# Attention block on one core: adding transfers moved in the issue order of GpSimd

## The chip, the core and the metric

The kernel runs on one core of a Trainium2 chip. A core has a matrix engine (TensorE, PE in the profile, with its weight loads shown as PEld), a vector engine (VectorE, DVE), an engine for activation functions (ScalarE, ACT), a general engine (GpSimd, POOL) and a queue engine that only issues transfers (SyncE, SP). Each engine takes its own instructions strictly in order, and they wait for each other by semaphores. Data lies in the on-chip memory (SBUF, 128 partitions) and in the accumulation banks of TensorE (PSUM). Sixteen transfer (DMA) engines move data; a transfer is issued by one of the engines' queues, and a transfer that adds to what lies at its destination is issued here by POOL.

The metric is device time of one execution in microseconds (us): 1025.42 us is the median of three runs before the change (1024.97 to 1025.84).

## The reference

One transformer layer over 1024 latent tokens (16 rows of 64) of width 1024, with 256 context tokens. The first half of the layer mixes tokens, half of its width by four pooling windows and half by attention over a neighbourhood of 8 x 16 tokens plus all context tokens, and projects the two halves together:

```python
h_x = _modulate(x, g_pre_mix[l], sh1, sc1)
u_x, q_x, k_x, v_x = _project(h_x, w_in[l])
attn_x = _neighbourhood_attention(q_x, k_x, v_x, k_c, v_c, rpb[l])
mix_x = jnp.concatenate([_pool_mixer(u_x, pool_w[l], pool_scale[l]), attn_x], axis=-1) @ w_out[l]
x = x + gt1 * _rmsnorm(mix_x, g_post_mix[l])
y_x = _sq_relu_mlp(_modulate(x, g_pre_mlp[l], sh2, sc2), w_mlp_in[l], w_mlp_out[l])
x = x + gt2 * _rmsnorm(y_x, g_post_mlp[l])
```

All is float32.

## The kernel before

**Arithmetic.** A float32 product is made as three products of rounded parts: each operand is split in a high part (a cast) and a low part (what the cast left, `low_part`, L175, a DVE instruction that reads two SBUF operands), and TensorE forms high x high, high x low and low x high (L221 to L223). The large projections are further done by a scheme of seven block products instead of eight, whose operands are sums and differences of blocks. Some of those sums are made by adding transfers: `add_to(to, more)` (L211) is a transfer issued by POOL which adds `more` to `to`.

**Stages.** From 0 to some 218 us: modulation, projections of pools, keys, queries and values. From 218 to 317 us: attention. Then the output projection to some 400 us, then the MLP.

**Attention.** There are 32 units: 4 pairs of heads (j) times 8 tiles of 128 tokens (m). The loop runs over i = 0 to 35, and in step i TensorE does in this order: the scores of unit i (L1168, tiles `S`, two buffers of two banks, one for each head e of the pair), the turning of unit i-2 (L1214, transposes of its weights `sp` and of its shares `rb` by multiplication with `ident`, into `T`, `pa`, `pz`), and the weighted values of unit i-3 (L1248). Around that:

- DVE adds the bias table to the scores and takes the row's minimum (L1183, `sp`, `nm`), for e = 0 and 1. Between the two it takes the reciprocal of the row sums of unit i-1 (L1198, `ri`).
- ACT takes the exponential (L1194), copies one half of the turned weights (L1233) and the small side pieces (L1228, `px`); DVE copies the other half (L1233, `pt`).
- POOL spreads the reciprocal over 128 columns (L1200, `rb`). This copy is issued inside `scores(i)` for unit i-1, and TensorE needs it when it turns that unit, in step i+1.
- POOL also builds bias tables (L1037, `tab`, from a loaded table `U`), splits operands (L1050, L1051), and issues transfers.
- DVE multiplies the values by the shares into `heads[j]` (L1258, `weighed`).

In steps 0 and 1 TensorE also finishes the query projection (`last_query("P4", i)`, tiles `pqv`), and in step 1 the queries are split (`query_parts(0, 1)`: ACT L169, DVE L175 with output `qP`).

**The adding transfers.** `pools[k]` (`y` in the profile) are four pages of 1024 columns, `s3[k]` their left and `s1a[k]` their right half. First `s3[k]` gets `s1a[k]` added (k = 0 to 3); SP copies the sums into `sa2[k]` (`ss`, L1403, steps 5 and 6). When pair j of heads is finished, its right half is added to `s1a[j]` and to `sa2[j]` (step 8j+11), and later `sa2[j]` to the left half of `heads[j]` (step 8j+15). Each moves 128 x 512 numbers, 256 KB. The sums are operands of the output projection.

**Order.** The engines' order here is the order in which the code is written: the manager `in_order` ties each instruction of an engine to the one before it (for POOL `first_pool`). So on POOL whatever stands ahead of a `rb` copy in the code is issued ahead of it. In step i the code before the change wrote the adding transfers ahead of `scores(i)`:

```python
if i > 3:
    weighed(i - 4)
    if i % 8 == 3: ...          # two adds of finished heads
...
if i in (1, 2): ...             # two adds each of the pools
if 8 < i < N and i % 8 == 7: ...# one add to the heads
low()
if i < N:
    scores(i)                   # holds the rb copy of unit i-1
```

Of the kernel before, what the change touches and what calls it, by code (L numbers as in the profile page):

```python
# [103 lines left out]
def hybrid_block(ctx, tc, x, ctx_in, w_mod, mod_pages, b_mod, gp1, gp2, w_in, pool_w, rpb, w_out, w1, w2, vectors,  # L104
# [105 lines left out]
    def add_to(to, more):  # L210
        nc.gpsimd.dma_start(to, more, accum_op=add)  # L211
# [82 lines left out]
    with tc.tile_pool(name="ps1", bufs=6, space=PSUM) as ps1, tc.tile_pool(name="tmp1", bufs=3) as tmp:  # L294
# [10 lines left out]
        ET = mybir.EngineType  # L305
# [747 lines left out]
        def part_page(name, spare):  # L1053
            return whl.tile([P, 1024], F32R, tag="hl", name=name) if spare else page(name, F32R)
# [7 lines left out]
        def query_parts(j, b, spare=False, pool=False):  # L1062
            t = part_page(f"qP{j}_{b}", spare)
            qparts[j, b] = t[:, :512], t[:, 512:]
            apart(qT[j][b], *qparts[j, b], pool)
# [73 lines left out]
    with (  # L1139
# [6 lines left out]
        probs, least, sums, shares, turns, turned, fifths, heads = {}, {}, {}, {}, {}, {}, {}, {}  # L1146
# [114 lines left out]
        N = len(units)  # L1261
# [66 lines left out]
        sa2 = [both[k // 2][:, (k % 2) * 512 : (k % 2) * 512 + 512] for k in range(4)]  # L1328

        s3, s1a = [p[:, :512] for p in pools], [p[:, 512:] for p in pools]  # L1330
# [12 lines left out]
        with in_order(ET.PE, ET.Activation, ET.DVE, ET.SP) as projected:  # L1343

            def last_query(n, j):
                half_product(n, "Q", j, last_queries)
                kept_product(n, "Q", j, last_queries[j])

            query_parts(0, 0, True)
            key_parts(0, 1)  # L1350
            query_parts(1, 0, True, True)
            last_query("P7", 0)
            last_query("P7", 1)

            table = [None] + [tables(j) for j in (1, 2, 3)]
            built = lambda j: next(table[j])
            out_of = lambda n: mod_out(n, accs[n])
            jobs = {0: [(built, 1), (key_parts, 1, 0), (key_parts, 1, 1)], 1: [(built, 1)], 2: [(built, 1)], 3: [(built, 1)],
                    4: [(built, 1)], 5: [(out_of, "a")], 6: [(out_of, "sc")], 7: [(query_parts, 1, 1, True, True)],
                    8: [(mixed_split, 0, True)], 9: [(built, 2), (out_of, "sh")],  # L1360
                    10: [(columns_of, "sc", scale2), (built, 2)], 12: [(columns_of, "sh", s2), (built, 2)],
                    13: [(built, 2), (built, 2)], 14: [(query_parts, 3, 0, False, True)],
                    16: [(mixed_split, 1, True)], 17: [(query_parts, 2, 1, True, True)],
                    18: [(built, 3), (key_parts, 3, 0, False, True)], 20: [(built, 3), (built, 3)],
                    21: [(built, 3), (built, 3)], 22: [(key_parts, 3, 1, False, True)], 24: [(mixed_split, 2, True)],
                    25: [(query_parts, 3, 1, False, True)], 26: [(weight_split, 0, True)], 28: [(weight_split, 1, True)],
                    29: [(weight_split, 2, True)], 30: [(weight_split, 3, True)]}
            for i in range(N + 4):
                if i in LOADS:
                    weight_load(0, kks[LOADS.index(i)])  # L1370
                if i == N:
                    t1 = [out_load(f"to1_{kk}w", kk, 1) for kk in (0, 1)]
                    b22 = [out_load(f"bo22_{kk}w", kk, 1) for kk in (2, 3)]
                    t3 = [out_load(f"to3_{kk}w", kk, 1) for kk in (2, 3)]
                    for to, kk in zip(t1, (0, 1)):
                        add_to(halved(to), out_block(kk, 0))
                if i == N - 2:
                    G1 = gate_page("a")
                if i > 3:
                    weighed(i - 4)  # L1380
                    if i % 8 == 3:
                        j = i // 8 - 1
                        add_to(s1a[j], heads[j][:, 512:])
                        add_to(sa2[j], heads[j][:, 512:])

                rest_of_bank = lambda name: pz[:, 256:]
                if i == 0:
                    gain = mod_gain(gp1, att.tile([P, 256], F32, tag="gp", name="gpa"), nc.sync)
                if i == 4:
                    mod_gate("a", accs["a"], gain, rest_of_bank)  # L1390
                    accs["sh"] = page("accsh2")
                    nc.sync.dma_start(accs["sh"], kept_row)
                if i == 5:
                    column_sums("sc", accs["sc"], rest_of_bank)
                if i == 8:
                    column_sums("sh", accs["sh"], rest_of_bank)
                if i in (1, 2):
                    with tc.issue_after(pooling[ET.Pool]):
                        for k in (2 * i - 2, 2 * i - 1):
                            add_to(s3[k], s1a[k])  # L1400
                if i in (5, 6):
                    for k in (2 * i - 10, 2 * i - 9):
                        nc.sync.dma_start(sa2[k], s3[k])  # L1403
                if 8 < i < N and i % 8 == 7:
                    j = i // 8 - 1
                    add_to(heads[j][:, :512], sa2[j])
                low()
                if i == N:
                    mixed_split(3)
                for n, at in enumerate(HALVES):  # L1410
                    if at == i:
                        weight_split(n)
                if i < N:
                    scores(i)
                    for f, *args in jobs.get(i, ()):
                        f(*args)
                else:

                    t = i - N
                    if t == 0:  # L1420
                        x, s1 = [], halves_of("so1_")
                    if t % 2 == 0:
                        xs = ps_s.tile([P, 1024], F32, tag="S", name=f"pox{t}")
                        x += [xs[:, :512], xs[:, 512:]]
                    out_sums(x[t], "A11", wo, t, True)
                    nc.scalar.copy(s1[t], x[t])
                if 1 < i <= N + 1:
                    turn(i - 2)
                    fifth_kept(i - 2)
                if i < N:  # L1430
                    exps(i, 0)
                if 1 < i <= N + 1:
                    turn_kept(i - 2, 0, nc.scalar.copy)
                if i < N:
                    exps(i, 1)
                if i == 0:
                    key_parts(2, 0, True, "lo")
                    key_parts(2, 1, True, "lo")
                    query_parts(2, 0, False, "lo")
                if 1 < i <= N + 1:  # L1440
                    turn_kept(i - 2, 1, nc.vector.tensor_copy)
                if i < 2:
                    last_query("P4", i)
                if i == N:
                    share(i - 1)
                if 2 < i <= N + 2:
                    values(i - 3)
                if i == 1:
                    query_parts(0, 1)
                if i > N:  # L1450
                    out_operand("S1", i - N - 1, s1a[i - N - 1])
            low()
            for t in range(4):
                out_sums(x[t], "A12", [wo[2], wo[3]], t, False)
            t2 = [out_load(f"to2_{kk}w", kk, 1, wraw) for kk in (2, 3)]
            t4 = [out_load(f"to4_{kk}w", kk, 0, wraw) for kk in (2, 3)]
            for i in range(2):
                add_to(t2[i], t1[i])
            add_to(heads[3][:, :512], sa2[3])
            for i in range(2):  # L1460
                add_to(halved(t3[i]), out_block(i, 1))
            for i in range(2):
                add_to(t4[i], t2[i])
            first_pool.__exit__(None, None, None)
            wt1 = [high_low(f"to1_{t}", t1[t]) for t in range(2)]
            junk = lambda t: att.tile([P, NKEY], F32, tag="sp", name=f"jo0_{t}", bufs=6)[:, :512]
            out_operand("S2", 0, sa2[0])
            out_kept(0, 0, x[0], junk(0))
            out_operand("S2", 1, sa2[1])
            out_operand("S1", 3, s1a[3])  # L1470
            out_kept(0, 1, x[1], junk(1))
            out_operand("S2", 2, sa2[2])
            out_operand("S2", 3, sa2[3])
            for t in (2, 3):
                out_kept(0, t, x[t], junk(t))
# [729 lines left out]
```

## Time and profile before

| | us |
|---|---|
| median of three runs | 1025.42 (1024.97 to 1025.84) |
| the profiled execution | 1025.65 |
| its span, first to last instruction | 1023.9 |
| PE busy | 1012.5 (99%) |
| DVE busy | 747.8 (73%) |
| ACT busy | 544.8 (53%) |
| POOL busy | 149.8 (15%) |
| granted clock of TensorE | 0.998 |

How to read it: the profile is one execution. Its busy times of TensorE are partly modelled, since matmuls are pipelined. A row of the timeline gives the start and the length of an instruction (or of several equal ones in a row, "x3"), and in brackets how long the engine had been idle and which instruction ended that wait. The chain that ended last goes back from the last instruction, at each step to what released it. Each `DMA_DIRECT2D` row on POOL is the time in which POOL issued a transfer, not the transfer's own time.

### The profile page before, as it was taken

Reading aid. Unit: us, or ns where it says so; the run is one execution under the profiler, and the core shown is the slowest. Engines: PE = TensorE matmul, PEld = TensorE weight load, DVE = VectorE, ACT = ScalarE, POOL = GpSimd, SP = SyncE. Lnnn points to the kernel's source line nnn. Section 1 sums busy time; section 2 is a strip of 40 time slices with the busy share of each in tenths; the row PEclk is TensorE's granted clock in tenths of the full one; section 3 lists DMA queues with packets and bytes.
Section 4 is the critical chain, followed back from the end, with each engine's and each line's share of the span. In section 5 each row is a group of like instructions: output and inputs, shape, how many; then the busy total and the mean of one; then the engine's idle time right before and its main releaser. Section 6 shows DMA issues by size and latency. Waiting matters only on the chain.

```text
span 1023.9 us, 16144 instructions
## 1 busy us (share of the span) xinstructions
PE 1012.5 (99%) x5962; PEld 838.5 (82%) x5962; DVE 747.8 (73%) x1164; ACT 544.8 (53%) x949; POOL 149.8 (15%) x231
## 2 busy tenths in 40 slices
PE   9999999999999999999999999999999999999997
PEld 7788888878898888888888888888888888888886
DVE  5688657977886688879998888755756666547576
ACT  6683254348886646776555554545543334334431
POOL 3011110156773321410000000000000000000002
PEclk9999999999999999999999999999999999999999
DMA  9899798623347955886776666537967766546555
GB/s 359 321 260 337 246 268 297 206 59 86 86 95 205 228 183 198 272 203 205 262 254 212 214 198 227 183 133 237 347 219 256 259 215 219 204 175 195 166 184 225
DMA packets 117023, 222.72 MB, mean 218 GB/s; under 512 B 9488, under 2 KB 46992, under 8 KB 116944
## 3 DMA queue, kind: packets, MB, share of 16 engines
q1 hardware_dynamic: 90448, 171.14, 49.5%
q0 software_dynamic: 9360, 19.58, 9.4%
q10 hardware_dynamic: 17136, 30.97, 8.1%
q8 instruction: 47, 0.77, 0.3%
q14 instruction: 32, 0.26, 0.1%
HBM read 168.16 MB, written 52.45 MB: 215 GB/s over the span
## 4 chain that ended last, share of the span: by engine, by line
PE 95%; DMA 2%; POOL 1%; ACT 1%; issue 0%; DVE 0%; SPq 0%; DVEq 0%; POOLq 0%; ACTq 0%
PE pu L467 4%; PE pa L1248 4%; PE phz L221 3%; PE phv L221 3%; PE phx L221 3%; PE pyx L221 3%; PE pyx L223 3%; PE phx L223 3%; PE pyv L222 3%; PE pyz L222 3%; PE phz L223 3%; PE pyx L222 3%; PE phv L223 3%; PE pyv L223 3%; PE pyz L223 3%; PE phx L222 3%
## 5 line engine op out<-in xcount | busy, mean ns | idle before, releaser
L1194 ACT ACTIVATE sp<-sp,nm 128x640 f32<-128x640 f32 (+1 forms) x64 | 51.5, 804 | 9.6 <-DVE ri L1198 4.9
L1183 DVE CUSTOM_DVE_ANT_0 sp<-S,tab 128x640 f32<-128x640 f32 (+1 forms) x56 | 44.6, 796 | 14.1 <-PE pz L1214 9.7
L169 ACT CAST wpS<-S 128x512 fp32r<-128x512 f32 x64 | 38.7, 616 | 29.0 <-PE phv L223 10.0
L1790 ACT ACTIVATE c<-c 128x512 f32<-128x512 f32 x48 | 30.3, 631 | 42.9 <-DVE c L1910 25.0
L221 PE MATMUL phx<-thB,wpA 128*128 128x512 f32 x128 | 50.2, 392 | 0.0
L223 PE MATMUL phx<-thB,wpA 128*128 128x512 f32 x128 | 49.8, 389 | 0.0
L222 PE MATMUL phx<-tlB,wpA 128*128 128x512 f32 x128 | 49.8, 389 | 0.0
L175 DVE TENSOR_TENSOR wpS<-S,wpS 128x512 fp32r<-128x512 f32 x64 | 43.5, 688 | 8.4 <-ACT wpS L169 8.4
L163 POOL TENSOR_TENSOR ry<-vy,nhalf 128x1 f32<-128x1 f32 x8 | 5.9, 739 | 281.1 <-DVE vy L161 281.1
L1791 ACT ACTIVATE c<-c 128x512 f32<-128x512 f32 x48 | 30.3, 631 | 15.2 <-DVE sa L1873 12.2
L221 PEld LDWEIGHTS phx<-thB,wpA 128*128 128x128 f32 x128 | 24.0, 188 | 5.4 <-ACT s L1841 0.5
L223 PEld LDWEIGHTS phx<-thB,wpA 128*128 128x128 f32 x128 | 24.0, 188 | 5.1
L222 PEld LDWEIGHTS phx<-tlB,wpA 128*128 128x128 f32 x128 | 24.0, 188 | 4.8
L1233 DVE COPY pt<-T 128x512 f32<-128x512 f32 x32 | 22.0, 686 | 5.8 <-PE T L1214 5.8
L1248 PE MATMUL pa<-pt,v 128*64 128x128 f32 x352 | 25.9, 279 | 0.2
L221 PE MATMUL phz<-thB,wpS 128*128 128x512 f32 x64 | 25.0, 391 | 0.0
L221 PE MATMUL phv<-thT,wpA 128*128 128x512 f32 x64 | 25.0, 391 | 0.0
L223 PE MATMUL phz<-thB,wpS 128*128 128x512 f32 x64 | 24.9, 389 | 0.0
L222 PE MATMUL phv<-tlT,wpA 128*128 128x512 f32 x64 | 24.9, 389 | 0.0
L222 PE MATMUL phz<-tlB,wpS 128*128 128x512 f32 x64 | 24.9, 389 | 0.0
L221 PE MATMUL phy<-thT,wpS 128*128 128x512 f32 x64 | 24.9, 389 | 0.0
L222 PE MATMUL phy<-tlT,wpS 128*128 128x512 f32 x64 | 24.9, 389 | 0.0
(1139 smaller groups left out, 3438.1 us busy)
## 6 DMA issues: line engine op xcount, KB each, us to landing
b<-in_w SPq DMA_DIRECT2D x64, 512.0 KB, 4.2
hrS<-hdS SPq DMA_DIRECT2D x32, 512.0 KB, 5.1
hrA<-hdA SPq DMA_DIRECT2D x24, 512.0 KB, 5.2
wm<-in_mod_pages SPq DMA_DIRECT2D x16, 512.0 KB, 9.6
wa_0w<-in_w SPq DMA_DIRECT2D x16, 512.0 KB, 5.2
wa_1w<-in_w SPq DMA_DIRECT2D x16, 512.0 KB, 4.4
hdA<-c ACTq DMA_DIRECT2D x32, 256.0 KB, 2.4
hdS<-sa ACTq DMA_DIRECT2D x32, 256.0 KB, 2.3
```

The source lines that it names most:

```text
L169: nc.scalar.copy(hi, src)
L175: nc.vector.tensor_tensor(lo, src, hi.bitcast(F32), sub)
L221: nc.tensor.matmul(ps, ahi, bhi, start=first, stop=False, skip_group_check=more)
L222: nc.tensor.matmul(ps, ahi, blo, start=False, stop=False, skip_group_check=more)
L223: nc.tensor.matmul(ps, alo, bhi, start=False, stop=last, skip_group_check=more)
L467: nc.tensor.matmul(pus[b][j], wk(wgt, k, low, j * P, P), r, start=(k == 0 and n == 0), stop=(k == KT - 1 and n == 2))
L1183: nc.vector.tensor_tensor_reduce(out=to, in0=s, in1=bt, scale=1.0, scalar=BIG, op0=add, op1=ALU.min, accum_out=nm)
L1194: nc.scalar.activation(sp, sp, AF.Exp, bias=least[i, e], scale=-1.0, accum_out=sums[i][:, e : e + 1])
L1233: copy(turns[i].rearrange("p e i t -> p (e i) t")[:, :, h * HD : (h + 1) * HD], turned[i][h].rearrange("p (a t) -> p a t", a=8))
L1248: nc.tensor.matmul(pa[e * HD : (e + 1) * HD, cols], v[:, f : f + HD], turns[i][:, e, c] if c < 4 else fifths[i][:, :, (e + 1) * HD : (e + ...
L1790: nc.scalar.activation(r, src, AF.Relu)
L1791: nc.scalar.activation(r, r, AF.Square)
```

## The change

Only POOL's order changes; the instructions, their number and their operands stay. Three groups of adding transfers move:

1. The four adds `s3[k] += s1a[k]` move from steps 1 and 2 to the place ahead of the last query products and of unit 0.
2. The two adds of finished heads in steps 11, 19 and 27 move behind `scores(i)`, which means behind the `rb` copy of unit i-1. (In step 35 there are no scores; they stay.)
3. The add to the left half of the heads in steps 15, 23 and 31 moves likewise.

```diff
             query_parts(1, 0, True, True)
+            with tc.issue_after(pooling[ET.Pool]):
+                for k in range(4):
+                    add_to(s3[k], s1a[k])
             last_query("P7", 0)
             last_query("P7", 1)
+
+            def right_added(j):
+                add_to(s1a[j], heads[j][:, 512:])
+                add_to(sa2[j], heads[j][:, 512:])
...
                     weighed(i - 4)
-                    if i % 8 == 3:
-                        j = i // 8 - 1
-                        add_to(s1a[j], heads[j][:, 512:])
-                        add_to(sa2[j], heads[j][:, 512:])
+                    if i > N and i % 8 == 3:
+                        right_added(i // 8 - 1)
...
-                if i in (1, 2):
-                    with tc.issue_after(pooling[ET.Pool]):
-                        for k in (2 * i - 2, 2 * i - 1):
-                            add_to(s3[k], s1a[k])
...
-                if 8 < i < N and i % 8 == 7:
-                    j = i // 8 - 1
-                    add_to(heads[j][:, :512], sa2[j])
                 low()
...
                     scores(i)
+                    if 8 < i and i % 8 == 3:
+                        right_added(i // 8 - 1)
+                    if 8 < i and i % 8 == 7:
+                        add_to(heads[i // 8 - 1][:, :512], sa2[i // 8 - 1])
```

What this does to POOL's order is seen at two places. The first is around units 0 to 2. Before the change POOL's rows are these (`y` are the pools' pages, `rb` the spread reciprocals of units 0 and 1, `tab` a bias table, `kP2l` and `qP` low parts of keys and queries):

```order
L1024 MEMSET tab_2182 128x256
L1024 MEMSET tab_2183 128x256
L1051 TENSOR_TENSOR kP2l<-kT_1885,kP2h 128x512 x2
L1051 TENSOR_TENSOR qP_0_2204<-q_2_1992,qP_0_2204 128x512
L211 DMA y_1367<-y_1367 128x512
L211 DMA y_1413<-y_1413 128x512
L1200 COPY rb_2241<-ri_2239 128x128
L1037 TENSOR_TENSOR tab_2182<-msk,U_2186 128x128 x3
L211 DMA y_1463<-y_1463 128x512
L211 DMA y_1503<-y_1503 128x512
L1200 COPY rb_2289<-ri_2287 128x128
```

After the change POOL's rows at the same place are these:

```order
L1051 TENSOR_TENSOR qP_0_2128<-q_0_1741,qP_0_2128 128x512
L211 DMA y_1367<-y_1367 128x512
L211 DMA y_1413<-y_1413 128x512
L211 DMA y_1463<-y_1463 128x512
L211 DMA y_1503<-y_1503 128x512
L1024 MEMSET tab_2186 128x256
L1024 MEMSET tab_2187 128x256
L1051 TENSOR_TENSOR kP2l<-kT_1885,kP2h 128x512 x2
L1051 TENSOR_TENSOR qP_0_2208<-q_2_1992,qP_0_2208 128x512
L1200 COPY rb_2243<-ri_2241 128x128
L1037 TENSOR_TENSOR tab_2186<-msk,U_2190 128x128 x3
L1200 COPY rb_2289<-ri_2287 128x128
```

The four issues went ahead of the memsets and of the splits of keys and queries, and nothing stands any more between the last split and the first `rb` copy, and only one table step between the first and the second.

The second place is POOL in step 11, as one piece of the difference (`f` are the finished heads, `sc` and `s` small columns of the modulation that POOL fetches):

```order
 L776 DMA sc_984<-gsc 128x8x1
 L1037 TENSOR_TENSOR tab_2029<-msk,U_2800 128x128 x3
+L1200 COPY rb_2933<-ri_2931 128x128
 L211 DMA y_1367<-f_2394 128x512
 L211 DMA ss_2119<-f_2394 128x512
-L1200 COPY rb_2935<-ri_2933 128x128
 L1200 COPY rb_3002<-ri_3000 128x128
 L776 DMA s_86<-gsh 128x8x1
```

The `rb` copy of unit 10 now goes ahead of the two issues. In steps 19 and 27 the same happens, and in steps 15, 23 and 31 with one issue. The rows of PE, DVE, ACT and SP are the same as before, in the same order.

## The prediction

> **What bounds the kernel now.** I read the page first, then who TensorE waited for over the whole span, then the timelines of PE, POOL and DVE at those waits.
>
> ```profile
> span 1023.9 us, 16144 instructions
> PE 1012.5 (99%) x5962; PEld 838.5 (82%) x5962; DVE 747.8 (73%) x1164; ACT 544.8 (53%) x949; POOL 149.8 (15%) x231
> PE 95%; DMA 2%; POOL 1%; ACT 1%; issue 0%; DVE 0%; SPq 0%; DVEq 0%; POOLq 0%; ACTq 0%
> ```
>
> TensorE is the bound: 95% of the chain that ended last, and only 11.4 us of its span idle. POOL is busy 15%, so moving its work can only pay where TensorE waits for POOL. The list of TensorE's waits names these, for attention:
>
> ```profile
> PE pa L1214 <- POOL rb L1200: 1.8, 3, 0.8
> PE S L1168 <- DVE nm L1183: 0.3, 1, 0.3
> ```
>
> Three waits, 1.8 us in all. PE's timeline shows where (rows before a wait show when PE was done):
>
> ```profile
> 226.96 0.29 PE L1168 MATMUL S<-kch,qP 64*128 64x256 f32 x2
> 227.87 0.27 PE L1214 MATMUL pa<-ident,rb 64*128 64x64 f32 x1 [0.62 <-POOL rb L1200]
> 229.18 0.44 PE L1168 MATMUL S<-kP0h,qP 64*128 64x384 f32 x1 [0.31 <-DVE nm L1183]
> 231.10 0.27 PE L1214 MATMUL pa<-ident,rb 64*128 64x64 f32 x1 [0.77 <-POOL rb L1200]
> 259.52 0.27 PE L1214 MATMUL pa<-ident,rb 64*128 64x64 f32 x1 [0.39 <-POOL rb L1200]
> ```
>
> These are the turnings of units 0, 1 and 10, in steps 2, 3 and 12. The chain shows what stood ahead of POOL's copies for units 0 and 1:
>
> ```profile
> 224.51 1.29 POOL qP L1051
> 225.79 1.72 POOL y L211 x2
> 227.52 0.30 POOL rb L1200
> 227.81 1.21 POOL tab L1037 x3
> 229.02 1.73 POOL y L211 x2
> 230.75 0.31 POOL rb L1200
> ```
>
> and for unit 10:
>
> ```profile
> 257.36 0.92 POOL y L211
> 258.28 0.90 POOL ss L211
> 259.18 0.31 POOL rb L1200
> ```
>
> All three waits end at an `rb` copy directly behind two issues that the change moves. No such wait is listed for steps 15 to 31, so moving those issues is worth nothing; the 0.9 us by which each delayed its copy was covered by TensorE's own work.
>
> **Part 1, the pools' adds.** Their new place on POOL follows the split that ends at 215.24:
>
> ```profile
> 213.53 1.71 POOL L1051 TENSOR_TENSOR qP<-q,qP 128x512 fp32r<-128x512 f32 x1
> 222.00 2.55 POOL L1051 TENSOR_TENSOR kP2l<-kT,kP2h 128x512 fp32r<-128x512 f32 x2 [6.25 <-ACT kP2h L1050]
> ```
>
> Four issues take 1.72 + 1.73 = 3.45 us, to 218.7; the two memsets behind them take what they took. POOL was idle 6.25 us here, waiting for ACT until 222.00, so about 2.8 us of cover are left. Without this cover, what exceeds it would delay the first `rb` copy one for one. The issues also wait for DVE to have read the pages' left halves (a group at L177); that is over at 210.4:
>
> ```profile
> 209.10 1.29 DVE L177 SCALAR_TENSOR_TENSOR mix<-y,mix 128x512 fp32r<-128x512 f32 x2 [1.04 <-ACT mix L171]
> ```
>
> Behind 222.00 POOL goes on as before to the end of `qP` at 225.80 and can then copy at once: unit 0's copy ends at 226.1, before PE wants it at 227.87 - 0.62 = 227.25. The three table steps end at 227.4, and unit 1's copy waits for its reciprocal:
>
> ```profile
> 226.19 0.69 DVE L1100 TENSOR_TENSOR q<-pqv,q 128x512 f32<-128x512 f32 x1 [1.33 <-PE pqv L223]
> 226.80 0.77 DVE L175 TENSOR_TENSOR qP<-q,qP 128x512 fp32r<-128x512 f32 x1
> 227.50 0.81 DVE L1183 CUSTOM_DVE_ANT_0 sp<-S,tab 128x640 f32<-128x640 f32 x1
> 228.24 0.15 DVE L1198 RECIPROCAL ri<-su 128x2 f32<-128x2 f32 x1
> 228.31 0.80 DVE L1183 CUSTOM_DVE_ANT_0 sp<-S,tab 128x640 f32<-128x640 f32 x1
> 229.04 0.08 DVE L1183 DVE_READ_ACCUMULATOR2_ANT nm<- 128x1 f32 x1
> ```
>
> It ends at 228.4, so the copy ends at 228.7, before PE wants it at 231.10 - 0.77 = 230.33.
>
> What is late next? The 0.62 us are not won. After unit 0's turning PE does the scores of unit 3, which need the score buffer that DVE frees at 229.12, and DVE's work up to there does not depend on that turning. PE only waits 0.93 instead of 0.31 us at 229.18. The 0.77 us at unit 1 are won: there nothing else is late.
>
> One cost is new. DVE's `qP` (L175) at 226.80, which lies on the way to 229.18, now meets POOL's table steps (226.1 to 227.4), where before it met issues and a copy. What that does is seen earlier:
>
> ```profile
> 205.26 1.61 DVE L177 SCALAR_TENSOR_TENSOR mix<-y,mix 128x512 fp32r<-128x512 f32 x2
> 204.60 3.80 POOL L1037 TENSOR_TENSOR tab<-msk,U0w 128x128 f32<-128x128 f32 x7
> L177 DVE SCALAR_TENSOR_TENSOR mix<-y,mix x4: 684/722/933, 205.3 to 209.7; 128x512 fp32r<-128x512 f32 x4
> ```
>
> Beside table steps two such DVE operations took 1.61 us, after them 1.29 (the row at 209.10); the slowest of the four took 0.93 against 0.68. Bounds: 0 (it is slowed no more than now) and 0.6 (it waits for all three table steps, 226.80 to 227.4). I take 0.93 - 0.68 = 0.25, the same pair of instructions. That delays unit 3's scores and so all behind them: 0.77 - 0.25 = 0.52 us won.
>
> [...]
>
> **The transfers of part 1.** They now run from some 216 us, beside the two loads of `U`, where the transfer engines had room; before, they filled 226 to 234:
>
> ```profile
> 216.00:218.00 2.00, 2.00 (x10) 1.50 (x8) 0.40 (x1) 1.14 (x2) 0.00 (x0) 1.00 0.23 48
> 228.00:230.00 2.00, 1.69 (x29) 1.43 (x29) 1.72 (x6) 1.83 (x6) 2.00 (x5) 1.00 1.10 186
> U<-in_rpb SPq DMA_DIRECT2D x2, 244.5 KB, 3.9
> ```
>
> (The last two columns of the stages are the transfers' busy share and GB/s; the `U` row is for 215 to 217.5, with its 3.9 us to landing.) POOL's table step needs the first `U` from 226.1 on; issued at 215.82 it may take 10 us. Cost nothing; the cover is 6 us. SP's copies into `ss` wait for these adds and come earlier; nobody waits for them.
>
> **Part 2, step 11.** Unit 10's copy follows the table steps at 257.36 and ends at 257.7; PE wants it at 259.52 - 0.39 = 259.13. All 0.39 us are won. The two issues then end near 259.5, before unit 11's copy, which waited for DVE until 260.23:
>
> ```profile
> 260.23 0.29 POOL L1200 COPY rb<-ri 128x128 f32<-128x128 f32 x1 [0.76 <-DVE ri L1198]
> ```
>
> **Sum.** -0.52 - 0.39 = -0.91 us. Behind it TensorE is busy almost without gaps to the end, and the other engines' waits hang on its progress, so I let the gain reach the end. The profiled execution (1025.65: span 1023.9 and 1.75 around it) would be 1024.7; the median, 0.23 below it, 1025.42 - 0.9 = 1024.5 us.
>
> **Rivals.**
>
> - *The chain's price.* The chain put 1.72 + 1.73 + 0.92 + 0.90 = 5.27 us on the moved issues; without them it would end at 1020.2. Against it: PE lay idle at these places 0.62 + 0.31 + 0.77 + 0.39 = 2.09 us only, and a gain above that has no source in the trace. Some larger gain is still possible, if the modelled busy time of PE hides waits.
> - *Nothing reaches the end.* DVE waits the full 0.6, which leaves 0.17 + 0.39, and the rest is lost where the output projection waits for transfers. For it speaks the first row below, DVE's wait for a summed block of output weights; against it, that this chain of transfers starts from buffers that TensorE frees and so moves with it. Time 1025.4.
> - *Slower: `U` lands late.* POOL stands at the table step between the copies of units 0 and 1 until `U` is there. It decides from 228.7 on (230.33 less 1.33 for the steps and 0.3 for the copy). The slowest transfer of the output weights `to_3w`, in the busiest stretch, took 15.5 us to landing (second row below); as the second `U` load's time, from 217.0, that is 232.5, so unit 1 turns at 234.1 instead of 231.10, and with step 11 the sum is +2.6: 1028.0. Against it: 3.9 us now, and four adds of the length seen do not fill 13 us.
>
> ```profile
> DVE mp L1317 <- DMA to_3w<-to_1w: 2.4, 1, 2.4
> DMA to landing us min/median/max: 7.1/11.1/15.5
> ```
>
> **How the numbers follow.** 0.2% (2.05 us) is about what a measurement of this kernel can tell from no change. Forecast (0.3 to 1.6 us won) 0.58; nothing reaches the end (within 0.3 us) 0.18; a larger gain like the chain's, over 2.05 us, 0.13; slower by a late `U`, or by other contention of that size, 0.11. So faster 0.13, same 0.76, slower 0.11. The range takes in the full 2.09 us of idle and a little of the chain's case below, and some loss above: 1023.0 to 1026.2.
>
> **What would show it.** Right: no `rb` wait of PE at units 0, 1 and 10; a wait of some 0.9 to 1.2 us for `nm` ahead of unit 3's scores; `qP` of DVE longer than 0.77; POOL's four issues between 215 and 219 and `kP2l` still at 222.00; PE's idle about 0.9 us less. Wrong: a wait for `U` at the first table step, the turnings of units 0 or 1 late for another reason, or a shift at 317 us that is gone at the end.

## The result, and the profile after

The changed kernel takes 1023.87 us (median of 22 runs, 1023.28 to 1024.47); the kernel before, run beside it, 1025.48 us (22 runs, 1024.93 to 1025.92). The ratio is 0.9986 with a 95% interval of 0.998 to 0.9992: 1.61 us less, or 0.16%. That is inside the predicted range and inside 0.2%, on the side that was forecast, but 1.8 times the 0.9 us forecast, and at the very edge of the 0.3 to 1.6 us that the prediction set down for its own account of the change.

The profiled execution after took 1023.28 us, that of before 1025.65. Its page begins, and sums up its chain:

```profile
span 1021.4 us, 16146 instructions
PE 1011.2 (99%) x5962; PEld 838.7 (82%) x5962; DVE 747.2 (73%) x1164; ACT 544.7 (53%) x949; POOL 151.0 (15%) x231
PE 96%; DMA 2%; DVE 0%; ACT 0%; issue 0%; SPq 0%; DVEq 0%; POOLq 0%; ACTq 0%
```

POOL is gone from the chain, and TensorE is idle 10.2 us instead of 11.4. The spans differ by 2.5 us, but not all of that belongs to the change. The first query matmul, far ahead of the first changed instruction, stands here in before and in after (one fence each):

```profile
212.61 0.39 PE L221 MATMUL pqv<-S3h,wQT3h 128*128 128x512 f32 x1
```

```profile
211.97 0.39 PE L221 MATMUL pqv<-S3h,wQT3h 128*128 128x512 f32 x1
```

So 0.64 us is scatter of the start; the same matmul lay between 211.87 and 212.35 in the ten other traces told of below, so the trace of before is the latest of them all, and the profiled execution after has the lowest of its 22 times. All shifts from here on are counted from this matmul. Counted so, the turnings of after come earlier by 0.83 us (unit 0), 1.24 (unit 1), 1.13 (units 2 and 9), 1.68 (unit 10), 1.74 (units 11 to 25) and 1.79 (unit 31), and the last instruction by 1.86. Of the 1.86 us, 1.68 are made at the places that the prediction named, and they reach the end.

In attention, the list of TensorE's waits has no `rb` any more, and the one for `nm` has grown from 0.3 us:

```profile
PE S L1168 <- DVE nm L1183: 0.8, 2, 0.5
```

PE's timeline around the turnings of units 0, 1 and 10:

```profile
226.28 0.29 PE L1168 MATMUL S<-kch,qP 64*128 64x256 f32 x2
226.40 0.21 PE L1214 MATMUL pa<-ident,rb 64*128 64x64 f32 x1
...
227.60 0.44 PE L1168 MATMUL S<-kP0h,qP 64*128 64x384 f32 x1 [0.48 <-DVE nm L1183]
228.41 0.44 PE L1168 MATMUL S<-kP0h,qP 64*128 64x384 f32 x1 [0.37 <-DVE nm L1183]
...
229.22 0.21 PE L1214 MATMUL pa<-ident,rb 64*128 64x64 f32 x1
229.27 0.28 PE L1168 MATMUL S<-kch,qP 64*128 64x256 f32 x1
...
229.52 0.70 PE L1214 MATMUL T<-ident,sp 64*128 64x64 f32 x14
...
257.09 0.28 PE L1168 MATMUL S<-kch,qP 64*128 64x256 f32 x2
257.20 0.22 PE L1214 MATMUL pa<-ident,rb 64*128 64x64 f32 x1
```

Look at the starts. Where nothing is waited for, the turning starts 0.12 us after the last pair of score matmuls (226.28 to 226.40), although that pair's row goes on to 226.57. At unit 1 the first transpose even starts a little ahead of the last score matmul (229.22 and 229.27). That detail decides the size of the gain, below.

POOL's and DVE's timelines at the same place:

```profile
214.54 3.58 POOL L211 DMA_DIRECT2D y<-y  x4
221.36 2.55 POOL L1051 TENSOR_TENSOR kP2l<-kT,kP2h 128x512 fp32r<-128x512 f32 x2 [2.67 <-ACT kP2h L1050]
...
225.12 0.28 POOL L1200 COPY rb<-ri 128x128 f32<-128x128 f32 x1
225.37 1.74 POOL L1037 TENSOR_TENSOR tab<-msk,U 128x128 f32<-128x128 f32 x3
227.69 0.29 POOL L1200 COPY rb<-ri 128x128 f32<-128x128 f32 x1 [0.58 <-DVE ri L1198]
```

```profile
226.12 0.68 DVE L175 TENSOR_TENSOR qP<-q,qP 128x512 fp32r<-128x512 f32 x1
```

The four issues fill POOL's old wait for ACT, which shrinks from 6.25 to 2.67 us; `kP2l` still starts 9.39 us after the first query matmul, as before. The table steps follow the copy without a wait for `U`. DVE's `qP` was not slowed: 0.68 us against 0.77 before. It was POOL's three table steps (the row `x3`) that took longer: 1.74 us, against 1.27 for the next three (from 227.94).

### The profile page after: what moved, and what is told of

Read it like the earlier page. It is cut to its first block, busy times and chain, and to the rows that moved or that the text cites. A ratio compares the mean times of both kernels' runs of the same rounds, so it can differ in the third digit from the quotient of the medians.

```text
span 1021.4 us, 16146 instructions
## 1 busy us (share of the span) xinstructions
PE 1011.2 (99%) x5962; PEld 838.7 (82%) x5962; DVE 747.2 (73%) x1164; ACT 544.7 (53%) x949; POOL 151.0 (15%) x231
## 4 chain that ended last, share of the span: by engine, by line
PE 96%; DMA 2%; DVE 0%; ACT 0%; issue 0%; SPq 0%; DVEq 0%; POOLq 0%; ACTq 0%
PE pu L467 4%; PE pa L1248 4%; PE S L1168 3%; PE phx L221 3%; PE pyx L221 3%; PE phv L221 3%; PE phz L221 3%; PE phv L222 3%; PE phz L222 3%; PE pyv L223 3%; PE pyx L222 3%; PE pyv L221 3%; PE pyz L223 3%; PE pyz L221 3%; PE phx L222 3%; PE phx L223 3%
```

## The experiments

Timing resolves about 0.9 us between two kernels of some ten runs each (the intervals below reach some 0.0009 to each side), so terms of half a microsecond are read from the shifts in the traces, and the times stand beside them.

Two questions came first: which of the two parts brought what, and whether it is POOL's order or the earlier transfers that does it.

**Part 1 alone.** The adds of finished heads went back to where before has them:

```diff
                 if i > 3:
                     weighed(i - 4)
-                    if i > N and i % 8 == 3:
-                        right_added(i // 8 - 1)
+                    if i % 8 == 3:
+                        j = i // 8 - 1
+                        add_to(s1a[j], heads[j][:, 512:])
+                        add_to(sa2[j], heads[j][:, 512:])
...
+                if 8 < i < N and i % 8 == 7:
+                    j = i // 8 - 1
+                    add_to(heads[j][:, :512], sa2[j])
```

> The pools' four adds ahead of unit 0, all other adds where they were before. Theory A (a turning of TensorE waits for POOL's copy, and its true stall is the listed idle time plus some 0.16 us, by which the modelled end of the last matmul outlasts its turn): -1.1 us against before (0.77 + 0.17 at unit 1 and 0.1 to 0.2 of DVE being done sooner ahead of unit 3's scores); unit 10's wait of 0.39 us is still listed. Theory B (the gain comes from the transfers leaving 226 to 234 us): the same here. By the prediction's own sum: -0.5 us.

It took 1024.74 us against 1025.59, ratio 0.9991 (0.9982 to 1.0). In its trace the turnings come 0.74 us earlier from unit 2 on, and the end 0.86, less than the 1.1 that theory A expected. Its DVE, POOL and PE rows, each from that engine's timeline:

```profile
226.35 1.03 DVE L175 TENSOR_TENSOR qP<-q,qP 128x512 fp32r<-128x512 f32 x1
```

```profile
225.57 1.27 POOL L1037 TENSOR_TENSOR tab<-msk,U 128x128 f32<-128x128 f32 x3
```

```profile
228.18 0.44 PE L1168 MATMUL S<-kP0h,qP 64*128 64x384 f32 x1 [0.83 <-DVE nm L1183]
```

Here DVE paid: POOL's three steps took 1.27 us, DVE's `qP` took 1.03 instead of 0.68, and the first wait for `nm` was 0.83 us instead of 0.48. That is where theory A's sum went. The code at this place is that of after. The collision that the prediction priced is real, but which side pays for it changes from execution to execution.

**Part 2 alone.** The pools' adds went back into steps 1 and 2, ahead of the scores:

```diff
-            with tc.issue_after(pooling[ET.Pool]):
-                for k in range(4):
-                    add_to(s3[k], s1a[k])
...
+                if i in (1, 2):
+                    with tc.issue_after(pooling[ET.Pool]):
+                        for k in (2 * i - 2, 2 * i - 1):
+                            add_to(s3[k], s1a[k])
```

> The adds of finished heads behind their unit's scores, the pools' adds as before. Theory A: the waits at units 0 and 1 stay (0.62 and 0.77 listed), unit 10's goes, -0.55 us in the trace from unit 10 on and nothing at the later units. The prediction's own sum: -0.39 us. Theory B: 0.

1025.04 us, ratio 0.9996 (0.9987 to 1.0005), which timing does not tell from before. In the trace nothing moves up to unit 9; unit 10's turning comes 0.54 us earlier, unit 11's 0.60, unit 31's 0.65. Steps 15 to 31 are thus worth 0.05 us at most. The list of waits keeps the two of units 0 and 1:

```profile
PE pa L1214 <- POOL rb L1200: 1.4, 2, 0.7
```

Part 2 is worth 0.54 to 0.60 us, though the wait that it removes was listed with 0.39.

**The pools' adds behind the scores.** POOL's copies go first, but the transfers keep their old time: the adds stay in steps 1 and 2, behind `scores(i)`, and the heads' adds stand as before. The edit is shown against the kernel before.

```diff
-                if i in (1, 2):
-                    with tc.issue_after(pooling[ET.Pool]):
-                        for k in (2 * i - 2, 2 * i - 1):
-                            add_to(s3[k], s1a[k])
...
                 if i < N:
                     scores(i)
+                    if i in (1, 2):
+                        with tc.issue_after(pooling[ET.Pool]):
+                            for k in (2 * i - 2, 2 * i - 1):
+                                add_to(s3[k], s1a[k])
```

> The pools' adds stay in steps 1 and 2, but behind the scores, so behind the copies of units 0 and 1; their transfers stay where they were, around 226 to 234 us. Theory A: -0.9 to -1.1 us against before, since the copy of unit 1 is ready at about 229.4 and TensorE wants it at 230.2. Theory B: no more than -0.4 us, since the transfers have hardly moved.

1024.09 us, ratio 0.9988 (0.9979 to 0.9997). The turnings come 1.10 us earlier at unit 1 and 1.0 from unit 2 on, the end 1.06. POOL's timeline:

```profile
225.00 0.30 POOL L1200 COPY rb<-ri 128x128 f32<-128x128 f32 x1
225.24 1.77 POOL L211 DMA_DIRECT2D y<-y  x2
```

So the gain of part 1 comes from the copies' place on POOL, not from earlier transfers: the rival of the transfers is refuted. Here two issues stand between the copy and the table steps, and `qP` took 0.79 us, about what it took before.

**Half of the pools' adds.** Adds 0 and 1 stay in step 1, ahead of the scores, so that unit 0's copy is late as before; adds 2 and 3 go ahead of unit 0.

```diff
             with tc.issue_after(pooling[ET.Pool]):
-                for k in range(4):
+                for k in (2, 3):
                     add_to(s3[k], s1a[k])
...
+                if i == 1:
+                    with tc.issue_after(pooling[ET.Pool]):
+                        for k in (0, 1):
+                            add_to(s3[k], s1a[k])
```

The heads' adds stand as before, too.

> Two of the pools' adds go ahead of unit 0, the other two stay ahead of unit 0's copy in step 1. Theory A: TensorE still waits some 0.6 us for the copy of unit 0, not for that of unit 1, and the gain is still -0.8 to -1.1 us, since unit 0's wait is covered by DVE ahead of unit 3's scores. If unit 0's wait counts for itself: about half of the gain of the whole move, -0.5 us. Theory B: about half as well, since half of the transfers have moved.

PE's timeline keeps unit 0's wait:

```profile
227.30 0.27 PE L1214 MATMUL pa<-ident,rb 64*128 64x64 f32 x1 [0.61 <-POOL rb L1200]
228.60 0.44 PE L1168 MATMUL S<-kP0h,qP 64*128 64x384 f32 x1 [0.31 <-DVE nm L1183]
```

Unit 0's turning does not move (0.01 us), unit 1's comes 1.12 us earlier, units 2 to 11 come 1.0 earlier, the end 1.04: about as much as where unit 0's wait was removed and `qP` not slowed (0.99 to 1.13 at unit 2). In the trace, removing unit 0's wait is worth nothing, as predicted: the time that it gives back is spent ahead of unit 3's scores. The timed runs do not confirm the whole: 1025.14 us (1024.13 to 1026.83), ratio 0.9998 (0.9989 to 1.0007), some 0.6 us above what the trace shows. Why they scattered more than others stays open. The two longest, 1026.13 and 1026.83 us, have a granted clock of 0.997, the other nine 0.998 or 0.999; that would fit a stretch at half clock like the one of 3.4 us seen with seven copies below (by estimate, half of 3.4 us is 0.0017 of the span), but no trace of these two was kept.

**The changed kernel once more.** Unchanged, for the outcome of the collision.

> The changed kernel again, beside the others of this group. -1.1 to -1.9 us against before: the part before 212 us scatters by some 0.6 us between executions, and DVE's qP (L175) takes 0.68 us or about 1.03 us, depending on whether it or one of POOL's table steps comes first; so the wait for nm ahead of unit 3's scores is 0.85 or 1.2 us in all.

1023.88 us, ratio 0.9985 (0.9976 to 0.9993). PE's waits in this execution:

```profile
228.01 0.44 PE L1168 MATMUL S<-kP0h,qP 64*128 64x384 f32 x1 [0.83 <-DVE nm L1183]
228.81 0.44 PE L1168 MATMUL S<-kP0h,qP 64*128 64x384 f32 x1 [0.36 <-DVE nm L1183]
```

`qP` took 1.03 us, and the shifts are 0.73 us for units 2 to 9, 1.27 at unit 10 and 1.38 at the end: 0.48 us less than in the other execution of the same program. The outcome of the collision thus differs between two executions of one program. POOL's third table step in after, where DVE's `qP` started at 226.12, and then both in this execution:

```profile
226.19 0.93 POOL L1037 TENSOR_TENSOR tab<-msk,U 128x128 f32<-128x128 f32 x1
```

```profile
226.18 1.03 DVE L175 TENSOR_TENSOR qP<-q,qP 128x512 fp32r<-128x512 f32 x1
226.21 0.45 POOL L1037 TENSOR_TENSOR tab<-msk,U 128x128 f32<-128x128 f32 x1
```

Exactly one of the two is held up each time: the table step by 0.48 us, or `qP` by 0.35.

**No table step beside qP.** The three table steps of step 1 go to step 2:

```diff
-            jobs = {0: [(built, 1), (key_parts, 1, 0), (key_parts, 1, 1)], 1: [(built, 1)], 2: [(built, 1)], 3: [(built, 1)],
+            jobs = {0: [(built, 1), (key_parts, 1, 0), (key_parts, 1, 1)], 2: [(built, 1), (built, 1)], 3: [(built, 1)],
```

> The changed kernel with the first three table steps taken from behind unit 0's copy to behind unit 1's, so that POOL is idle while DVE makes qP (L175). If the collision of the two costs time (the prediction's term of 0.25 us): L175 takes 0.68 us in every execution, the wait for nm ahead of unit 3's scores is 0.85 us in all, and the time is 0 to 0.35 us below that of the changed kernel. If it costs nothing: L175 0.68 us and the same time.

It was run again later, beside the last experiment:

> The kernel with the first table built in steps 2 and 3 once more, as the comparison for the one with the gate's sums in step 3. By both theories 1023.8 within 0.5, qP of DVE (L175) 0.68 us since no table step of POOL lies beside it, and the end 1.6 to 1.8 us ahead of the kernel before against the first query matmul. A qP of 1.03 us here would refute that the table steps are what slows it.

1023.8 us, ratio 0.9983 (0.9974 to 0.9991), and 1023.5 us, ratio 0.9982 (0.9973 to 0.9991). `qP` took 0.68 us both times, the first wait for `nm` 0.48, and the ends come 1.74 and 1.75 us earlier. The table steps are what slows `qP`; without them it took 0.68 us in each of three traces, these two and that of the last experiment. By time alone this version is not told from the changed kernel: the difference is 0.08 us beside the unchanged repeat.

**What a listed wait is worth.** The two removed waits that paid, at units 1 and 10, had been worth more than listed. To measure that by itself, units 13 to 28 copy their reciprocals seven times, so that PE waits for POOL at nearly each of these turnings:

```diff
-            (nc.gpsimd if i < N - 1 else nc.vector).tensor_copy(
-                shares[i].rearrange("p (e t) -> p e t", e=2),
-                ri.rearrange("p (e o) -> p e o", o=1).to_broadcast([P, 2, HD]))
+            for _ in range(7 if 13 <= i < 29 else 1):
+                (nc.gpsimd if i < N - 1 else nc.vector).tensor_copy(
+                    shares[i].rearrange("p (e t) -> p e t", e=2),
+                    ri.rearrange("p (e o) -> p e o", o=1).to_broadcast([P, 2, HD]))
```

> The changed kernel, but POOL makes the copies of the shares of units 13 to 28 seven times each (the same values), so that TensorE must wait for them. Theory A: the attention part becomes longer than the idle time listed for the turnings by about 0.16 us for each wait; with 16 waits the time grows by some 2.5 us more than the sum of the listed waits. Rival (the listed idle time is the whole stall): the growth equals the sum of the listed waits within 0.5 us.

1044.58 us, ratio 1.0186 (1.0172 to 1.02). The list of waits, and two turnings on PE's timeline (the copy's lines are one higher here):

```profile
PE pa L1215 <- POOL rb L1201: 15.9, 14, 1.6
```

```profile
277.71 0.29 PE L1168 MATMUL S<-kch,qP 64*128 64x256 f32 x2
279.21 0.27 PE L1215 MATMUL pa<-ident,rb 64*128 64x64 f32 x1 [1.21 <-POOL rb L1201]
```

From 277.71 to 279.21 are 1.50 us; unstalled it is 0.12, so the stall is 1.38, and 1.21 are listed. Over the whole stretch, I compared the spacing of the turnings with that of the unchanged repeat. The 14 listed waits sum to 15.9 us. Thirteen of them list 15.63, and the spacings at these thirteen grew by 17.93, that is 0.18 us more per wait on average (0.02 to 0.24 at single ones). Two units with no listed wait grew by 0.25 us each. One unit, 21, grew by 2.00 us where 0.24 are listed; there TensorE's clock had been halved from 297.38 on (0.69 in the microsecond from 297.00), behind a wait of 1.61 us (its windows: PE, PEld, DVE, ACT and POOL busy, then the granted clock, the transfers' share, GB/s):

```profile
296.77 0.27 PE L1215 MATMUL pa<-ident,rb 64*128 64x64 f32 x1 [1.61 <-POOL rb L1201]
```

```profile
296.00:297.00 1.00, 0.23 (x6) 0.23 (x8) 0.83 (x5) 0.00 (x0) 0.88 (x4) 1.00 0.00 0
298.00:299.00 1.00, 1.00 (x12) 1.00 (x12) 0.55 (x1) 1.00 (x4) 1.00 (x3) 0.50 0.00 0
299.00:300.00 1.00, 1.00 (x12) 0.72 (x8) 0.00 (x0) 0.85 (x3) 0.88 (x4) 0.50 0.00 0
```

17.93 + 0.50 + 2.00 = 20.4 us is the whole growth up to unit 31 (20.4 in the trace; 20.7 by the medians). The rival, that a listed wait is the whole stall, is refuted: it is a lower bound, on average 0.18 us short at a turning here. (The whole growth beyond the 15.9 us listed is 4.5 us; 2.3 of it stands at the thirteen waits, where theory A had 2.5 at sixteen, and the rest is the two units without a listed wait and the halved clock.)

**Filling the wait for `nm`, twice.** What is left ahead of unit 3's scores is 0.48 + 0.37 us of waiting. In the changed kernel the four column sums of the gate page (L259) were moved into it from step 4, and a query job of DVE behind it:

```diff
-                if i == 4:
+                if i == 3:
                     mod_gate("a", accs["a"], gain, rest_of_bank)
+                if i == 4:
...
-                if i == 1:
+                if i == 2:
                     query_parts(0, 1)
```

> The changed kernel with the eight matmuls of the gate's sums (L259 on acca, 0.57 us on TensorE) moved from step 4 to step 3, into the wait for nm ahead of unit 3's scores, and the second half of the queries of the first pair split one step later, which takes L175 off DVE's way to those scores. Theory A: that wait of 0.85 us and more shrinks to 0.3 us or less, and the time is 0.5 to 0.9 us below that of the changed kernel. If the wait only moves to DVE's copies of the turned weights, 0 to 0.2 us.

1026.81 us, ratio 1.001 (1.0001 to 1.0019): some 1.3 us slower than before the change, which neither forecast had. Timelines of PE and DVE, and windows of 1 and 2 us:

```profile
231.61 0.37 PE L1214 MATMUL pz<-ident,rb 64*128 64x64 f32 x1 [1.87 <-DVE acca L270]
231.88 1.16 PE L1214 MATMUL T<-ident,sp 64*128 64x64 f32 x16
```

```profile
230.53 0.69 DVE L175 TENSOR_TENSOR qP<-q,qP 128x512 fp32r<-128x512 f32 x1 [1.38 <-ACT qP L169]
231.14 0.42 DVE L270 TENSOR_TENSOR acca<-pz,gpa 128x256 f32<-128x256 f32 x1
```

```profile
230.00:231.00 1.00, 0.00 (x0) 0.00 (x0) 0.47 (x1) 0.49 (x1) 0.00 (x0) 0.92 0.05 20
230.00:232.00 2.00, 0.39 (x8) 0.39 (x10) 1.47 (x3) 0.49 (x1) 0.00 (x0) 0.71 0.03 10
232.00:234.00 2.00, 2.00 (x29) 1.88 (x27) 1.79 (x6) 1.87 (x6) 1.47 (x4) 0.50 0.00 0
```

The sums share the tile `pz` with unit 1's turning, so the turning waits until DVE has read them (L270). On DVE that read now stood behind the moved `qP`, which itself waited for ACT. One wait of 1.87 us came of it, and before it was over the clock fell to half (0.92 in the microsecond from 230.00: it fell at 230.84), for 6.8 us (to 237.66: 0.67 in the microsecond from 237.00): the 16 matmuls into `T` took 1.16 us, 0.66 at the same turning in before. The turnings of unit 9 came 2.80 us later than before.

To see which of the two moves did that, the sums alone were moved, in the version without table steps beside `qP`:

```diff
-                if i == 4:
+                if i == 3:
                     mod_gate("a", accs["a"], gain, rest_of_bank)
+                if i == 4:
```

> As the kernel that builds the first table with steps 2 and 3 (no table step of POOL beside qP), with one more change: the four column sums of the gate page (PE L259, 0.57 us) and their product (DVE L270) stand in step 3 instead of step 4; the queries stay where the change has them. Theory (a wait is worth what lies behind it, and can be filled with work of PE that needs nothing late): the sums run in PE's wait for nm ahead of unit 3's scores, which were 0.48 + 0.37 us; that wait shrinks to some 0.3 us, L270 runs in DVE's idle 0.52 us behind the copy of unit 0, unit 1's turning stays where it is within 0.1 us, and unit 2's turning comes 0.4 to 0.6 us earlier against the first query matmul than in the kernel without this; the end too, some 2.2 us ahead of the kernel before, 1023.3. Rival (what made the kernel with the moved queries slow was the sums' product on the shared tile pz itself): a wait of PE for acca at L1214 again, over 0.5 us, and the turnings from unit 2 on later than without this. TensorE's granted clock stays 1.00 in this stretch by both.

1023.0 us (1022.72 to 1023.5), ratio 0.9975 (0.9965 to 0.9985): 2.5 us faster than before, and 0.5 faster than the same version without this move (1023.5 beside it), which by time alone is too little to tell. PE and DVE:

```profile
227.06 0.64 PE L259 MATMUL pz<-acca,ones 128*32 128x256 f32 x8
227.63 0.44 PE L1168 MATMUL S<-kP0h,qP 64*128 64x384 f32 x1
228.41 0.44 PE L1168 MATMUL S<-kP0h,qP 64*128 64x384 f32 x1 [0.35 <-DVE nm L1183]
```

```profile
228.88 0.41 DVE L270 TENSOR_TENSOR acca<-pz,gpa 128x256 f32<-128x256 f32 x1
229.50 0.82 DVE L1183 CUSTOM_DVE_ANT_0 sp<-S,tab 128x640 f32<-128x640 f32 x1 [0.20 <-PE pa L1214]
```

The sums fill the 0.48 us wait, their read fits into DVE's idle time, and unit 2's turning comes 1.64 us earlier than in before, where it was 1.09 without this move; the end comes 2.33 us earlier, against 1.75 without it. Sums on the shared tile do no harm by themselves. That the moved query job did it is read from the trace of the first, where `qP` stands ahead of the sums' read; no run moved that job alone. This version has the lowest median of all.

## Why the prediction was right, and where its sizes were off

The same places, in us against the kernel before (minus is won), by the prediction's terms. Unit 3's scores are the second of the two rows with a wait for `nm` (in before the one at 229.18): 16.57 us after the first query matmul before, 16.44 in after, 16.82 in its repeat.

| term | forecast | after | its repeat |
|---|---|---|---|
| unit 3's scores (`qP` against table steps) | +0.25 | -0.13 | +0.25 |
| from there to unit 2's turning (unit 1's wait) | -0.77 | -1.00 | -0.98 |
| unit 10 (step 11) | -0.39 | -0.55 | -0.54 |
| behind that, to the end | 0 | -0.18 | -0.11 |
| sum | -0.91 | -1.86 | -1.38 |

- *Unit 0's wait is worth nothing.* Right by the traces: the half of the pools' adds that keeps this wait moves unit 2 by 1.01 us, the changes that remove it by 0.99 to 1.13 where `qP` is not slowed; the times of that experiment, 0.45 us below before, leave it unconfirmed. The wait for `nm` that takes its place was forecast at 0.93 us plus what `qP` loses; it was 0.85 with a fast `qP` and 1.19 with a slow one.
- *The sizes of the waits won.* The step that failed is "The 0.77 us at unit 1 are won" and, with it, "All 0.39 us are won". The mechanism held; the terms were mis-sized. The idle time of a listed wait begins at the modelled end of the last matmul, but unstalled the next one starts 0.12 us after that matmul's start, inside its row. From the rows of before themselves: 227.87 - 226.96 = 0.91, less 0.12, is 0.79 at unit 0, listed 0.62. At unit 10, whose last scores started at 258.85, it is 0.67 - 0.12 = 0.55, listed 0.39, and 0.54 to 0.55 were won. At unit 1 the last row of before starts at 230.04: 1.06 - 0.12 = 0.94, listed 0.77, and 1.0 was won. The last 0.06 come from the spacing: in after this turning starts before the last score matmul does, so 0.12 is too much for it. Its last transposes into `T` end 1.95 us behind the start of that score row in before (231.99) and 0.95 in after (230.22), which is the 1.00 won. The lengthened copies show the same, 0.18 us per wait. The prediction's rival of a larger gain said that modelled busy time might hide waits, and then gave that case no term in the sum. The two rows of before that this rests on:

```profile
230.04 0.28 PE L1168 MATMUL S<-kch,qP 64*128 64x256 f32 x1
...
258.85 0.28 PE L1168 MATMUL S<-kch,qP 64*128 64x256 f32 x2
```

- *The collision of `qP` with the table steps.* The forecast of 0.25 us lay between the bounds 0 and 0.6 and was taken from one pair of rows. It is not one number, but comes out one of two ways. In one execution of this code `qP` took 0.68 us, 0.09 less than before, and the third table step 0.93; in three others (part 1 alone, the repeat and the seven copies, which share the code up to here) `qP` took 1.03 and that step 0.45. What goes with the outcome is small: `qP` started 14.15 us after the first query matmul in the one, 14.18 to 14.19 in the three. In the repeat, the term came out at the forecast's 0.25 to the hundredth. That is luck: the pair of rows was another DVE instruction (L177), and its 0.25 was a loss against 0.68 us, while `qP` took 0.77 in before. That 0.77 was itself not free: where POOL issued transfers beside it `qP` took 0.75 to 0.79 us (before, part 2 alone, the adds behind the scores, half of the adds), and where POOL did nothing 0.68. In each of the four executions with table steps beside `qP`, exactly one of the two was held. That this depends on which of them comes first, as the expectation for the repeat had it, was the author's estimate and is not shown: by the starts of the rows `qP` is ahead of the third table step in all four, by 0.07 us in the one and by 0.03 to 0.04 in the three. The upper bound, all three table steps, was not seen: 1.03 - 0.68 = 0.35 us, less than one table step of 1.27 / 3 = 0.42.
- *Step 11 alone counts in part 2.* Right: at most 0.05 us for steps 15 to 31.
- *The rivals.* "Nothing reaches the end" is refuted: shifts made at 231 and 257 us are there at the end. "U lands late" is refuted: the table steps began right behind unit 0's copy in every trace of this order. The chain's 5.27 us were not to be had. The moved transfers cost nothing, as forecast: with the moved adds the transfers' busy share is 1.04 to 1.12 in the stretches of 216 to 222 us (two of the three are shown), and TensorE is busy throughout:

```profile
216.00:218.00 2.00, 2.00 (x15) 1.45 (x16) 0.39 (x1) 0.71 (x2) 2.00 (x5) 1.00 1.04 146
220.00:222.00 2.00, 2.00 (x15) 1.49 (x15) 1.56 (x3) 2.00 (x6) 0.64 (x1) 1.00 1.12 236
```

- *The signs named.* No `rb` wait, a grown wait for `nm`, four issues in POOL's gap, `kP2l` in its place: all seen. "`qP` longer than 0.77" was seen in three of four executions and missed in the one shown as after. PE's idle time fell by 1.2 us, not 0.9.

The forecast's sum of -0.91 with the three corrections (0.16 more at unit 10, some 0.2 more at unit 1, and `qP` at -0.13 or +0.25) gives -1.7 or -1.3 before the 0.1 to 0.2 us behind unit 10, which no term accounts for. The median of the timed runs, -1.61, lies between the two executions' -1.86 and -1.38.

## What to carry to other kernels

The idle time listed for a matmul was a lower bound here, 0.18 us short on average at thirteen lengthened waits: measure a stall from start to start, and subtract the spacing that the same pair has where nothing waits. Before removing a wait, name what is late next; unit 0's wait bought nothing, and the place where the time went could then be filled with matmuls that need nothing late, which was worth as much again as step 11. When filling it, follow the tile that the moved work shares and everything queued ahead of the engine that must read it.

## What was not expected of the hardware

- Two instructions on DVE and POOL that meet at the same place of the same code came out either way between executions here: `qP` 0.68 us with the three table steps at 1.74, or 1.03 with them at 1.27. That alone moves this kernel by 0.38 us at unit 3's scores.
- TensorE's clock fell to half at short waits: in the kernel with the gate's sums and the query job moved, inside a wait listed with 1.87 us (0.92 in the microsecond from 230.00, 0.50 after it), and with seven copies 0.6 us behind one of 1.61, but not after ones of 1.41, 1.40 and 1.31 there (the 16 matmuls into `T` behind each of these took 0.66 us, as in before). In the first, the clock fell at 230.84, when TensorE had started nothing for 1.4 us (the last scores started at 229.46, the turning at 231.61, 2.15 us later). Unit 9's turning came 3.9 us later than in after (2.80 + 1.13), of which the stall itself explains some 2.0; the rest goes with the halved clock. The eleven times of that kernel run from 1024.67 us at a mean granted clock of 0.998 to 1027.55 at 0.995, so the fall is not the same in each. With seven copies TensorE had started nothing from 294.87 to 296.77, for 1.90 us, and the clock fell at 297.38, when it was at work again. The half clock lasted 6.8 us in the one trace and 3.4 in the other (297.38 to 300.80, with 0.60 in the microsecond from 300.00). Why the clock fell at these waits and not at the others stays open.
